# Sparse and cross attention: the low parts of the keys in both halves of the rows

## The chip, the cores and the metric

The kernel runs on one core of one Trainium2 chip. The metric is the device time of one execution in microseconds (us), the median of the runs shown; lower is better. Five engines work side by side, each on its own instruction queue: TensorE (PE; its weight loads are listed apart as PEld), VectorE (DVE), ScalarE (ACT), GpSimd (POOL) and SyncE (SP), which here only issues DMAs.

## The reference, cut to what matters

Two transformer blocks run one after the other on 256 tokens of width 1024, all in float32. The first block has a pooling mixer, a block attention and a gated MLP. The second has two layers, each with a mixer, a cross attention to 256 memory rows, an output projection with layer norm, and a mixture of 16 experts (MoE). The mixer of layer 0 is a sparse attention (NSA: 12 query heads of width 64, 4 key heads, a compressed, a selected and a window branch, mixed by gates); that of layer 1 is a latent attention (MLA). What this change is about is the scores:

- NSA, for each of 12 heads: the query times the keys of the selected and of the window branch, `s = (q · k) * 0.125`, causal, softmax, times the values, times the gate of the branch.
- Cross attention, in each layer, 4 heads of width 64: `s = (xq · mem_k) * 0.125`, softmax over the 256 memory rows, times `mem_v`.

## The kernel before, in words

**Split products.** TensorE takes a float32 product in two ways here: as float32 in several passes, or as fp32r in one pass with fewer bits. To keep the accuracy at one pass, an operand is split into a high part (its fp32r rounding) and a low part (what is left): `put_split` makes the high part with a copy (`copy`, on ACT or DVE, whichever the planner finds sooner) and the low part with a subtraction (`tt`, on DVE or POOL). A projection adds three products, high by high, high by low and low by high (`mm3`).

**Scores of heads of width 64.** A head has 64 rows, and the array has 128. `nsa_queries` (line 1480) and `cross` (line 1312) therefore put the high part of the query into one half of the rows and its low part into the other half, in one tile `qs`. `nsa` (line 1429) and `cross_keys` (line 1301) put the high part of the keys into both halves of `kh`. One matmul over 128 rows then gives high by high and low by high at once. A second matmul, over the 64 rows that hold the high query, multiplies it with the low part of the keys, `kl`, which lies in that half alone:

```python
nc.tensor.matmul(sv, q[:, i % 3, kv % 2, ts_], kh[:, kv, :, :nk], start=True, stop=False)
nc.tensor.matmul(sv, q[r, i % 3, kv % 2, ts_], kl[r, kv // 2, :, :nk], start=False, stop=False)
```

In `nsa_pair` (line 1500) a score group is these two and two bf16 matmuls that add the causal mask; a group covers 128 queries (`qt` is 0 or 1) and, for both branches at once, 2x128 or 2x256 keys. There are 12 heads and two groups each: 24 groups. In `cross`, `pair(j)` makes two groups, and each holds two heads: 128 rows, 64 rows, 128 rows, 64 rows, with 256 keys each. There are two pairs in each of two layers: 8 groups.

**Behind a score** stands `attend` (line 901): a maximum on DVE, small DVE operations, two exponentials on ACT, a reciprocal, two scalings (ACT, DVE or POOL), transposes on PE, a copy, and then the products with the values.

**The order of the work** is made by a planner in the kernel itself (class `Plan`): all operations are recorded in program order with an estimate of their time (`cost`), and `order` puts them on the engines one after the other, taking at each step the operation that can start first, with a preference for those that are due early (`rank`). `group()` keeps the matmuls of a group together. `filler(later)` makes what is recorded in it due later, so that it fills holes: in `nsa` that is, among others, the values, `cross_keys(0)`, the compressed branch and the second half of the queries; in `mla` `cross_keys(1)` and two thirds of the queries. `turn` books 0.19 us on PE where a matmul has at most 64 rows and the one in front of it has more, or the other way round, and 0.095 us for such a change in the columns. Where the planner sees a hole of over 0.6 us on PE, it puts matmuls on a dummy tile (`busy`, line 972 in the profile) into it, so that the engine stays busy. A tile's place in the arena (208 units of 256 columns) is given when its first operation is ordered; a DMA of MoE weights (512 KB, 4 units) is ordered when there is room for it.

Of the kernel before, what the change touches and what calls it, by code (L numbers as in the profile page):

```python
# [11 lines left out]
F32 = mybir.dt.float32  # L12
F32R = mybir.dt.float32r
# [3 lines left out]
OP = mybir.AluOpType  # L17
AX = mybir.AxisListType

S = 256  # L20
# [627 lines left out]
class K:  # L648
# [652 lines left out]
    def cross_keys(self, l):  # L1301

        mk = self.mem[l][0]
        kh, kl = self.mid([2, 2, S], F32R), self.mid([2, S], F32R)
        for j in range(2):
            r, o = self.halves(j), self.halves(1 - j)
            self.copy(kh[r, j], mk[r])
            self.tt(kl[r], mk[r], kh[r, j].bitcast(F32), OP.subtract)
            self.copy(kh[o, j], mk[r])
        return kh, kl  # L1310

    def cross(self, l, xq, keys, mixT):

        nc = self.nc
        mv, (kh, kl) = self.mem[l][1], keys
        qs = self.mid([2, 2, S], F32R)
        for j in range(2):
            r, o = self.halves(j), self.halves(1 - j)
            self.copy(qs[r, j], xq[r])
            self.tt(qs[o, j], xq[r], qs[r, j].bitcast(F32), OP.subtract)  # L1320

        def pair(j):
            r = self.halves(j)

            def score(qt):
                sv, ts_ = self.ps().rearrange("p (i k) -> p i k", i=2), slice(qt * 128, qt * 128 + 128)
                with nc.group():
                    for s in range(2):
                        nc.tensor.matmul(sv[:, s], qs[:, j, s, ts_], kh[:, j, s], start=True, stop=False)
                        nc.tensor.matmul(sv[:, s], qs[r, j, s, ts_], kl[r, s], start=False, stop=True)  # L1330
                return sv
            pt = self.attend(score, (256, 256), 0.125)
            o = self.ps()
            with nc.group():
                for kt in range(2):
                    for s in range(2):
                        h = 2 * j + s
                        nc.tensor.matmul(o[64 * s:64 * s + 64, :S], mv[:, kt, h * 64:h * 64 + 64], pt[:, s, 2 * kt:2 * kt + 2],
                                         start=(kt == 0), stop=(kt == 1))
            self.put_split(o[:, :S], mixT[0][:, 6 + j], mixT[1][:, 6 + j])  # L1340
        for j in range(2):
            pair(j)
# [86 lines left out]
    def nsa(self, x):  # L1429

        nc, A, h = self.nc, self.A, self.h
        W = A["nsa_w_in"]


        kh, kl = self.big([4, 2, S], F32R), self.mid([2, 2, S], F32R)
        kf = [self.mid([2, S]) for _ in range(2)]
        for br, c0 in ((0, 768 + 512), (1, 768 + 1024)):
            self.feat(W, c0, 256, h, lambda j, p: self.rope(p, kf[j][:, br], self.Cn, self.Sn, S))
        for j in range(2):
            for s in range(2):  # L1440
                r, o = self.halves(s), self.halves(1 - s)
                self.copy(kh[r, 2 * j + s], kf[j][r])
                self.tt(kl[r, j], kf[j][r], kh[r, 2 * j + s].bitcast(F32), OP.subtract)
                self.copy(kh[o, 2 * j + s], kf[j][r])
        q = [self.nsa_queries(0, W, h)]

        wg = self.load(W[:, 2304:2340].rearrange("(k p) f -> p k f", p=128), [8, 36])
        wv = self.split(wg, [8, 36])
        p = self.ps()
        for kk in range(2):  # L1450
            with nc.group():
                for k in range(4 * kk, 4 * kk + 4):
                    self.mm3(p[:36, :S], (wv[0][:, k], wv[1][:, k]), (h[0][:, k], h[1][:, k]), k == 0, k == 7)
        gT, gates = self.sml(), self.stay([128, 2, 12, 3], "gates")
        nc.scalar.activation(gT[:36], p[:36, :S], AF.Sigmoid)
        p = self.ps()
        with nc.group():
            for t in range(2):
                nc.tensor.transpose(p[:, t * 36:(t + 1) * 36], gT[:36, t * 128:(t + 1) * 128], self.ident[:36, :36])
        self.copy(gates, p[:, :72].rearrange("p (t h b) -> p t h b", t=2, h=12))  # L1460
        vs, xq = self.mid([2, 2, 256]), self.mid([2, S])
        with nc.filler(self.LATE):
            for br, c0 in ((0, 768 + 768), (1, 768 + 1280)):
                self.tok256(W, c0, h, lambda t, p: self.copy(vs[:, br, t], p))
            keys = self.cross_keys(0)
            kcz, vb = self.compressed(W, h)
            q.append(self.nsa_queries(1, W, h))
            self.feat(W, 2340, 256, h, lambda j, p: self.copy(xq[:, j], p), heads=True)
        mixT = self.hilo()
        for c in range(2):  # L1470
            PcT = self.sml()
            self.compressed_probs(c, q[c][0], kcz, gates, PcT)
            for j in range(3 * c, 3 * c + 3):
                self.nsa_pair(j, c, q[c][1], kh, kl, gates, PcT, vb, vs, mixT)
        self.cross(0, xq, keys, mixT)
        return self.out_ln(0, mixT)
# [23 lines left out]
    def nsa_pair(self, j, c, q, kh, kl, gates, PcT, vb, vs, mixT):  # L1500
        nc = self.nc
        PTs, heads = [], []
        for s in range(2):
            hd = 2 * j + s
            i = hd - 6 * c
            kv = hd // 3
            heads.append((i, kv))
            r = self.halves(kv % 2)

            def score(qt):  # L1510
                nk = 128 * (qt + 1)
                sv = self.ps().rearrange("p (i k) -> p i k", i=2)[:, :, :nk]
                with nc.group():
                    ts_ = slice(qt * 128, qt * 128 + 128)
                    nc.tensor.matmul(sv, q[:, i % 3, kv % 2, ts_], kh[:, kv, :, :nk], start=True, stop=False)
                    nc.tensor.matmul(sv, q[r, i % 3, kv % 2, ts_], kl[r, kv // 2, :, :nk], start=False, stop=False)
                    for b in range(2):
                        nc.tensor.matmul(sv[:, b, nk - 128:], self.identb, self.causalb, start=False, stop=(b == 1))
                return sv
            PTs.append(self.attend(score, (128, 256), 0.125, coef=lambda qt: gates[:, qt, hd, 1:3]))  # L1520
        o = self.ps()
        with nc.group():
            for s, (i, kv) in enumerate(heads):
                nc.tensor.matmul(o[64 * s:64 * s + 64, :S], vb[:96, c, i], PcT[:96], start=True, stop=False)
            for b in range(2):
                self.pv_causal(o, [vs[:, b, :, kv * 64:kv * 64 + 64] for _, kv in heads], [PTs[s][:, b] for s in range(2)],
                               start=False, stop=(b == 1))
        self.put_split(o[:, :S], mixT[0][:, j], mixT[1][:, j])
# [489 lines left out]
```

## Time and profile before

| | |
|---|---|
| Median of 3 runs | 1085.08 us (1084.48 to 1088.63) |
| The profiled execution | 1079.5 us, of which 1077.8 us are the span from the first to the last instruction |
| Mean granted TensorE clock | 0.993 |
| Busy share of the span | PE 97%, PEld 65%, DVE 54%, ACT 38%, POOL 6% |
| HBM read | 290.60 MB, 271 GB/s over the span |

The shares are means over stages with different limits: block 1 and its MLP last to about 320 us, NSA with cross attention and output to about 505 us, the first MoE to about 740 us, MLA with cross attention and output to about 840 us, the second MoE to the end. Matmuls are pipelined and their ends are modelled, so that a busy PE isn't one at its peak: what a matmul holds the engine for is read from one start to the next. Nearly every instruction is issued in one helper and has its line, L639; groups are told apart by tiles and shapes.

### The profile page before, as it was taken

The page shows a single profiled execution, that of the slowest core. Times are in us where ns is not written, and L with a number is a line of the kernel's source. Part 1 is how long each engine was busy: PE and PEld are TensorE (multiplying, and loading weights), DVE is VectorE, ACT ScalarE, POOL GpSimd, SP SyncE. Part 2 cuts the span into 40 slices and gives each one's busy share as a digit, 9 for nine tenths or more (in the row PEclk, how much of TensorE's full clock was granted, in tenths as well). Part 3 has the DMA queues.
Part 4 walks back from the last instruction along what each step waited for, and adds up shares of the span by engine and source line. Part 5 has one row for each costly group of instructions (what it writes and reads, how often), then busy time and mean ns, then how long its engine had stood idle before and what let it go on. Part 6 is the DMA issues. An engine that isn't in the chain of part 4 may idle for free. (4 is left out here: it accounts for less than half of the span.)

```text
span 1077.8 us, 16501 instructions
## 1 busy us (share of the span) xinstructions
PE 1047.4 (97%) x6169; PEld 696.5 (65%) x6169; DVE 580.1 (54%) x1514; ACT 412.0 (38%) x957; POOL 64.2 (6%) x68
## 2 busy tenths in 40 slices
PE   9999999999999999999999999999999999999995
PEld 5987999999988887777333443436877434443431
DVE  7699997867765899885221111107995412110103
ACT  4484673534344566574211111215763312111211
POOL 0231100000010000200000000002200100000000
PEclk9999999999999999899999999999999999999998
DMA  9995235464676441287999999999677799999994
GB/s 309 362 330 199 95 117 178 146 223 164 243 235 199 172 157 60 70 292 262 333 387 374 368 387 367 365 350 378 226 258 272 245 385 371 363 387 379 355 356 149
DMA packets 172356, 292.83 MB, mean 272 GB/s; under 512 B 9251, under 2 KB 59340, under 8 KB 172268
## 3 DMA queue, kind: packets, MB, share of 16 engines
q1 hardware_dynamic: 172268, 291.69, 77.1%
q8 instruction: 51, 0.84, 0.3%
q14 instruction: 37, 0.30, 0.1%
HBM read 290.60 MB, written 1.06 MB: 271 GB/s over the span
## 5 line engine op out<-in xcount | busy, mean ns | idle before, releaser
L639 PE MATMUL ps<-span,span 128*128 128x256 f32 (+6 forms) x5432 | 948.7, 397 | 6.2 <-DVE span L639 3.0
L639 PEld LDWEIGHTS ps<-span,span 128*128 128x128 f32 (+2 forms) x5432 | 624.0, 173 | 305.2 <-issue 238.0
L639 DVE TENSOR_TENSOR span<-span,span 128x512 fp32r<-128x512 f32 (+6 forms) x415 | 244.9, 631 | 20.4 <-ACT span L639 18.4
L639 ACT CAST span<-span 128x512 fp32r<-128x512 f32 (+5 forms) x320 | 166.0, 574 | 23.6 <-DVE span L639 11.1
L639 DVE TENSOR_TENSOR span<-ps,span 128x512 fp32r<-128x512 f32 (+3 forms) x104 | 56.6, 550 | 176.4 <-ACT span L639 110.1
L639 DVE SCALAR_TENSOR_TENSOR span<-span,tiny,ps 128x512 f32<-128x512 f32 x16 | 12.0, 747 | 192.8 <-PE ps L639 192.8
L639 POOL TENSOR_TENSOR span<-span,span 128x512 fp32r<-128x512 f32 (+4 forms) x37 | 49.5, 1351 | 968.5 <-ACT span L639 592.0
L639 ACT COPY span<-ps 128x512 f32<-128x512 f32 (+3 forms) x109 | 53.1, 495 | 134.1 <-PE ps L639 119.5
L639 ACT CAST span<-ps 128x512 fp32r<-128x512 f32 (+1 forms) x67 | 34.2, 513 | 164.3 <-PE ps L639 150.1
L639 PE MATMUL ps<-cst,span 128*128 128x128 f32 (+1 forms) x363 | 59.5, 283 | 10.9 <-DVE span L639 8.8
L639 ACT ACTIVATE span<-ps 128x512 f32<-128x512 f32 (+3 forms) x33 | 18.5, 561 | 113.3 <-PE ps L639 113.0
L639 PEld LDWEIGHTS ps<-cst,span 128*128 128x128 f32 (+1 forms) x363 | 40.0, 141 | 30.5 <-DVE span L639 16.9
L639 ACT ACTIVATE span<-span 128x256 f32<-128x256 f32 (+4 forms) x36 | 16.1, 451 | 98.7 <-DVE span L639 94.9
L639 ACT ACTIVATE span<-ps,tiny 128x256 f32<-128x256 f32 (+3 forms) x94 | 42.9, 467 | 21.5 <-DVE tiny L639 17.0
L639 ACT ACTIVATE span<-ps,vecs 128x256 f32<-128x256 f32 (+2 forms) x62 | 29.4, 511 | 53.8 <-PE ps L639 53.5
L639 ACT ACTIVATE span<-span,tiny 128x256 f32<-128x256 f32 (+3 forms) x59 | 30.2, 531 | 20.4 <-DVE tiny L639 20.2
L639 DVE TENSOR_REDUCE tiny<-ps 64x1 f32<-64x2 f32 (+3 forms) x78 | 30.3, 393 | 12.2 <-PE ps L639 10.4
L972 PE MATMUL ps<-busy 128*128 128x512 bf16 x122 | 30.7, 404 | 1.4 <-POOL busy L968 1.4
L639 DVE TENSOR_SCALAR span<-ps,vecs 128x256 f32<-128x256 f32 (+2 forms) x25 | 13.1, 526 | 32.8 <-ACT span L639 32.6
L639 DVE CAST span<-span 128x512 fp32r<-128x512 f32 (+7 forms) x79 | 29.4, 381 | 2.1 <-DMA span<-in_w_in_dram 1.0
L639 PE MATMUL ps<-span,cst 8*128 8x512 f32 (+1 forms) x48 | 25.5, 625 | 0.0
L639 DVE SCALAR_TENSOR_TENSOR span<-span,vecs,span 128x255 f32<-128x255 f32 (+2 forms) x52 | 24.4, 481 | 0.7
(106 smaller groups left out, 368.5 us busy)
## 6 DMA issues: line engine op xcount, KB each, us to landing
span<-in_moe_w_gate_dram SPq DMA_DIRECT2D x128, 512.0 KB, 6.5
span<-in_moe_w_up_dram SPq DMA_DIRECT2D x128, 512.0 KB, 7.7
span<-in_moe_w_down_dram SPq DMA_DIRECT2D x128, 512.0 KB, 6.8
span<-in_w_up_dram SPq DMA_DIRECT2D x22, 1024.0 KB, 5.2
span<-in_w_out_dram SPq DMA_DIRECT2D x12, 1024.0 KB, 10.5
span<-in_w_down_dram SPq DMA_DIRECT2D x11, 1024.0 KB, 5.1
span<-in_w_in_dram SPq DMA_DIRECT2D x7, 1024.0 KB, 9.6
span<-in_nsa_w_in_dram SPq DMA_DIRECT2D x7, 1024.0 KB, 8.3
```

What stands on the lines that cost most here:

```text
L639: getattr(eng, op)(*[real(x) for x in a], **{n: real(x) for n, x in k.items()})
L972: return lambda: nc.nc.tensor.matmul(nc.banks[bank], busy[:, :128], busy, start=True, stop=True)
```

## The change

The low part of the keys is put into both halves of the rows, and the second matmul of a score goes over all 128 rows. It then adds the high and the low part of the query, each times the low part of the keys. For this `kl` in `nsa` becomes two tiles of [2, 2, 256] (one for each pair of key heads) in place of one, and in `cross_keys` it becomes [2, 2, 256] in place of [2, 256]. A copy to the other half comes after each subtraction: four in `nsa`, two in each call of `cross_keys`. The number of matmuls, their columns and their order within a group stay as they were.

```diff
@@ cross_keys
-        kh, kl = self.mid([2, 2, S], F32R), self.mid([2, S], F32R)
+        kh, kl = self.mid([2, 2, S], F32R), self.mid([2, 2, S], F32R)
         for j in range(2):
             r, o = self.halves(j), self.halves(1 - j)
             self.copy(kh[r, j], mk[r])
-            self.tt(kl[r], mk[r], kh[r, j].bitcast(F32), OP.subtract)
+            self.tt(kl[r, j], mk[r], kh[r, j].bitcast(F32), OP.subtract)
             self.copy(kh[o, j], mk[r])
+            self.copy(kl[o, j], kl[r, j].bitcast(F32))
         return kh, kl
@@ cross
-            r = self.halves(j)
-
...
-                        nc.tensor.matmul(sv[:, s], qs[r, j, s, ts_], kl[r, s], start=False, stop=True)
+                        nc.tensor.matmul(sv[:, s], qs[:, j, s, ts_], kl[:, j, s], start=False, stop=True)
@@ nsa
-        kh, kl = self.big([4, 2, S], F32R), self.mid([2, 2, S], F32R)
+        kh, kl = self.big([4, 2, S], F32R), [self.mid([2, 2, S], F32R) for _ in range(2)]
...
                 self.copy(kh[r, 2 * j + s], kf[j][r])
-                self.tt(kl[r, j], kf[j][r], kh[r, 2 * j + s].bitcast(F32), OP.subtract)
+                self.tt(kl[j][r, s], kf[j][r], kh[r, 2 * j + s].bitcast(F32), OP.subtract)
                 self.copy(kh[o, 2 * j + s], kf[j][r])
+                self.copy(kl[j][o, s], kl[j][r, s].bitcast(F32))
@@ nsa_pair
-            r = self.halves(kv % 2)
...
-                    nc.tensor.matmul(sv, q[r, i % 3, kv % 2, ts_], kl[r, kv // 2, :, :nk], start=False, stop=False)
+                    nc.tensor.matmul(sv, q[:, i % 3, kv % 2, ts_], kl[kv // 2][:, kv % 2, :, :nk], start=False, stop=False)
```

## Rows read from the trace of the kernel before

**Rows 1.** The page: busy time of each engine; the chain that ended last.
```profile
PE 1047.4 (97%) x6169; PEld 696.5 (65%) x6169; DVE 580.1 (54%) x1514; ACT 412.0 (38%) x957; POOL 64.2 (6%) x68
...
issue 9%; PE 4%; DMA 1%; POOLq 0%; DVE 0%; DVEq 0%
```

**Rows 2.** Busy time by stretch: stretch, length, each engine, clock, DMA share, GB/s.
```profile
60.00:100.00 40.00, 40.00 (x238) 31.84 (x237) 39.88 (x108) 24.80 (x59) 10.79 (x13) 1.00 0.83 274
...
390.00:420.00 30.00, 29.35 (x257) 24.47 (x256) 26.55 (x106) 17.19 (x54) 1.45 (x1) 1.00 0.18 61
...
450.00:480.00 30.00, 29.73 (x204) 20.98 (x205) 26.80 (x88) 22.82 (x79) 4.51 (x4) 1.00 0.76 264
...
760.00:832.00 72.00, 71.01 (x465) 58.26 (x464) 57.38 (x155) 40.90 (x120) 6.69 (x5) 1.00 0.72 252
```

**Rows 3.** Timeline of PE, NSA: start, length, instruction, first shape, count.
```profile
400.08 3.11 PE L639 MATMUL ps<-span,span 128*128 128x256 f32 x24
403.03 0.27 PE L639 MATMUL ps<-cst,span 128*128 128x128 f32 x1
...
416.00 0.90 PE L639 MATMUL ps<-span,span 128*128 128x512 f32 x2
416.84 0.29 PE L639 MATMUL ps<-bfs 128*128 128x128 bf16 x2
416.93 0.68 PE L639 MATMUL ps<-span,span 128*128 128x256 f32 x2
417.54 0.28 PE L639 MATMUL ps<-bfs 128*128 128x128 bf16 x2
...
477.29 11.05 PE L639 MATMUL ps<-span,span 128*128 128x512 f32 x50
488.18 1.03 PE L639 MATMUL ps<-cst,span 128*128 128x128 f32 x8
```

**Rows 4.** PE's 64-row matmuls by shape: two of 300 to 520, one of 720 to 860.
```profile
L639 PE MATMUL ps<-span,span 64*128 64x256 f32 x20 | 8.0, 400 | 0.0
...
L639 PE MATMUL ps<-span,span 64*128 64x512 f32 x12 | 6.2, 520 | 0.0
...
L639 PE MATMUL ps<-span,span 64*128 64x256 f32 x8 | 3.0, 380 | 0.0
```

**Rows 5.** Timeline of PE: two score groups of the first cross attention.
```profile
466.66 2.55 PE L639 MATMUL ps<-span,span 128*128 128x256 f32 x8
469.14 1.09 PE L639 MATMUL ps<-cst,span 128*128 128x128 f32 x8
```

**Rows 6.** Timeline of PE, NSA: where PE stood or was kept busy.
```profile
365.72 2.55 PE L972 MATMUL ps<-busy 128*128 128x512 bf16 x11
369.23 0.69 PE L639 MATMUL ps<-span,span 128*128 128x256 f32 x2 [0.96 <-DVE span L639]
...
389.20 0.41 PE L639 MATMUL ps<-cst,span 128*128 128x128 f32 x2 [1.40 <-DVE span L639]
...
441.20 0.77 PE L639 MATMUL ps<-cst,span 128*128 128x128 f32 x2 [1.03 <-ACT span L639]
```

**Rows 7.** 361 to 366: its busy time by engine, and its 64-row copies.
```profile
361.00:366.00 5.00, 5.00 (x43) 4.84 (x42) 4.83 (x11) 4.52 (x9) 0.00 (x0) 1.00 0.00 1
...
L639 ACT CAST span<-span 64x512 fp32r<-64x512 f32 x6 | 3.7, 619 | 0.4 <-DVE span L639 0.3
...
L639 DVE CAST span<-span 64x512 fp32r<-64x512 f32 x2 | 0.8, 422 | 0.0
```

**Rows 8.** Busy time by stretch, where the clock fell.
```profile
440.00:445.00 5.00, 3.97 (x15) 2.31 (x13) 3.52 (x19) 2.54 (x7) 0.36 (x1) 0.56 0.00 0
445.00:450.00 5.00, 5.00 (x31) 4.40 (x30) 3.41 (x16) 2.85 (x14) 0.00 (x0) 0.76 0.00 0
```

**Rows 9.** Busy time by stretch: before the first MoE, and in it.
```profile
505.00:510.00 5.00, 4.99 (x36) 3.49 (x35) 4.66 (x16) 2.41 (x5) 0.00 (x0) 1.00 0.05 8
520.00:720.00 200.00, 198.17 (x922) 78.62 (x920) 28.94 (x56) 31.71 (x57) 2.49 (x2) 1.00 1.02 371
```

## The prediction

> **What bounds the kernel now.** I read the page first: PE is busy 97% of the span, no other engine over 54%, and the chain that ended last is PE, "issue" and a little DMA [rows 1]. So an amount of PE time taken out can count, if PE is what the stage waits for. That is read stage by stage, from the busy times by stretch [rows 2]. In NSA, 390 to 420 us and 450 to 480, PE is busy 29.35 and 29.73 of 30 us, but DVE stands close behind it, at 26.55 and 26.80, while ACT has 17.19 and 22.82. From 760 to 832, which holds the second cross attention, PE has 71.01 of 72, DVE 57.38, ACT 40.90. Both stages are PE's by a short head in NSA and a long one in MLA. Since a busy PE may be one that waits inside a modelled matmul, I then read the timeline of PE from start to start.
>
> There the reader is to see a gap in rate. In a projection, 24 matmuls of 256 columns over 128 rows go by from 400.08 to 403.03, 0.123 us each, and 50, mostly of 512 columns, from 477.29 to 488.18, 0.218 us each [rows 3]. A score pair of the same columns, 128 rows and then 64 rows, takes 416.84 − 416.00 = 0.84 us for two of 512 columns and 417.54 − 416.93 = 0.61 us for two of 256 [rows 3]. In cross attention, where the two kinds alternate, 8 matmuls of 256 columns take 469.14 − 466.66 = 2.48 us, 0.310 each [rows 5]. Nothing is waited for in these groups, as no idle time is listed. What the slow ones have in common is a change between 128 and 64 rows: it costs 0.84 − 2 x 0.218 = 0.404 us for two changes, 0.61 − 2 x 0.123 = 0.364 for two, and 0.310 − 0.123 = 0.187 for one.
>
> **The change, part by part.** *The changes of rows go.* Of the 20 matmuls of 64 rows and 256 columns in the NSA stage 12 are NSA's short groups and 8 cross attention's; the 12 of 512 columns are NSA's long groups; 8 more stand in the second cross attention [rows 4]. So: 12 x 0.404 = 4.8 us, 12 x 0.364 = 4.4, 16 x 2 x 0.187 = 6.0, which halves into 3.0 for each layer. PE is relieved of 4.8 + 4.4 + 3.0 = 12.2 us in the NSA stage and of 3.0 in MLA, 15.2 together. The matmuls themselves cost the same: their columns and their number stay, and the 128-row ones of the projections are the price that I have put in.
>
> Here a rule speaks against the change. What the rows show is that a pair of 128 and 64 rows holds PE longer than two of 128 rows, and not shorter, in all three kinds of group [rows 3, 5]. The Trainium skill, "TensorEngine Tiling (Array Packing)", When to Use Tiling, advises tiles of 64 rows for contractions of up to 64, for up to twice the speed; by it, giving the low products all 128 rows is a step back. The same page, Key Properties, says that a change of the tiling mode drains the array, and with that the 0.187 us agree. By the first rule the low products would lose up to half of their streaming time, an estimate of 12 x 0.109 + 28 x 0.062 = 3.0 us; by the second the sum stays as above.
>
> *How much of the 12.2 us NSA keeps.* Its lower end is nothing: DVE could be what the stage then waits for. Its upper end is 12.2. What DVE allows, if no operation leaves it, is its idle time: 3.45 + 3.20 us in the two stretches of 30 [rows 2] and 1.48 + 1.59 between 440 and 450 [rows 8], 9.7 in all of the 70 us. DVE can run full: 39.88 of 40 us from 60 to 100 [rows 2]. And part of its work, copies and scalings, can go to ACT, which has 7 to 13 idle us in each stretch of 30. The holes of PE that are there already won't shrink, as they end on DVE and ACT: 2.55 of dummy matmuls and 0.96, then 1.40, then 1.03 [rows 6]. I take 8.1, two thirds, which is nearest to what DVE's own idle time allows, less some for the chains in which maximum, exponential and scaling follow each other.
>
> *The four copies in NSA.* One takes 0.62 us on ACT or 0.42 on DVE [rows 7]. They fall where the keys are split, 361 to 366, and there DVE is busy 4.83 of 5 us and ACT 4.52 [rows 7]. Two engines that share them need about 4 / (1/0.42 + 1/0.62) = 1.0 us. Behind them on both queues wait the ropes and splits of the first queries, and for those PE waits: the dummy matmuls and the hole before 369.23 [rows 6]. So they cost 1.0, at the most 4 x 0.62 = 2.5, and 0 if the planner slips them behind the queries; the first score needs them only at 369.
>
> *The two copies of each `cross_keys`* are due late and have ACT's idle time for cover, at worst 4 x 0.62 = 2.5 us for both layers if ACT were full. I take 0.
>
> *The room.* Four more units stand taken through NSA and two more from each `cross_keys` on, of 208. What waits for room are the loads of the MoE weights, 4 units each. One load fewer in advance is 0.5 MB at 371 GB/s, 1.4 us [rows 9]. Between 505 and 510 the DMA share is 0.05 [rows 9]: the loads stand complete before the MoE starts, and NSA's keys are free by then. So 0, at worst twice 1.4. No DMA is added or moved, on SP's queue or POOL's.
>
> *MLA.* PE relieved of 3.0 us; DVE has 14.6 idle us of 72 there. I take 2.5, between 0 and 3.0.
>
> **The sum.** −8.1 + 1.0 − 2.5 = −9.6 us. Against the profiled execution, 1079.5, that is 1069.9. The median of the runs shown lies 5.6 above that execution, and so I put the median after at 1085.08 − 9.6 = 1075.5.
>
> **The rivals.**
>
> *A. DVE and the chains take over (0.17).* PE then waits where it worked. For it: DVE is at 88% in NSA, and every hole there ends on DVE or ACT [rows 6]. Against it: ACT's idle time and DVE's 39.88 of 40 elsewhere. NSA would keep perhaps 2 of its 12.2, less 1.0 for the copies: with MLA's 2.5 some −3.5, 1081.6.
>
> *B. The MoE takes it back (0.06).* Its weights come at 371 GB/s with a DMA share of 1.02 [rows 9]; an earlier start helps only if the loads start earlier too. Against it: they were complete at 505 with time to spare. MoE would return all of NSA's 7.1, leaving 2.5: 1082.6.
>
> *C. The clock falls more often (0.10), the case on the slower side.* After PE stood 1.03 us before 441.20 [rows 6], with thin work around it, the granted clock was 0.56 and then 0.76 of full for 5 us each, the lower level of 1.2 GHz for part of the time [rows 8]: 5 x 0.44 + 5 x 0.24 = 3.4 us, with the hole 4.4. A PE that is done sooner while DVE is not has more such holes, and they lie where the late fillers are used up, 440 to 470. With four more of them than before: 4 x 4.4 − 9.6 = +8.0, 1093.1. Up to two they leave it level, from four on it is slower by over 0.5%. For it: the clock did fall there once. Against it: the planner fills the holes that it foresees, and full matmuls in place of drained ones keep PE denser. The Trainium skill, "TensorE: Matmul & The Clock Gate", Part 1, has it that the lower rate is the default and that steady work releases the higher one; the trace agrees, with these two stretches.
>
> *D. The change doesn't remove the slow steps (0.03).* If a second matmul on the same bank with the same weights were slow for another reason, 128 rows would not help; and if 64 rows had been the cheaper form, they would cost up to half of the low products' streaming, 12 x 0.218 / 2 + 28 x 0.123 / 2 = 3.0 us, more. Against it: the projections add to one bank, too, at 0.123 [rows 3]. Then the copies count and up to 3.0: +1.0 to +4.0, 1086.1 to 1089.1. (That is the time that the skill's page on array packing would give.)
>
> **How the numbers follow.** The forecast has 0.64 and reaches from all that the rows allow, −15.2 + 0 (1069.9), to a gain of 5.4 (1079.7). A new order is also planned from the first changed operation on, and that moves holes like those of [rows 6] by some us either way, so the low end goes to 1067. At the top A, B and the cheap end of D lie within, up to 1086.1, and I stop at 1087; C and the rest of D above it and a little below 1067 are left out. About 0.5%, 5.4 us, is what a measurement of this kernel can tell from no change. Faster by more is the forecast, 0.64; within it are A, B and D, 0.26; slower is C, 0.10.
>
> **What would show it.** In the profile after, no matmul of 64 rows is left from 300 to 520 and from 720 to 860; a score pair in NSA takes about 0.44 and 0.25 us from start to start, and the 8 of cross attention about 1.0. The first score comes about 1 us later than 369.23, the first MoE's stretch starts some 7 us earlier, the second's some 10. It is wrong in size if PE's idle time and dummy matmuls between 360 and 500 grow by more than about 5 us, and wrong in sign if the clock falls in several stretches there.

## The result, and the profile after

The changed kernel takes 1073.86 us, the median of 4 runs (1070.42 to 1075.42). The kernel before, run beside it, takes 1084.78 (4 runs, 1083.28 to 1088.63). The ratio is 0.9889, with a 95% interval of 0.9866 to 0.9912: 1.1% faster. The forecast was 1075.5, in a range of 1067 to 1087. The profiled execution takes 1070.42, with a span of 1068.7, which is 9.1 less than the profiled one before.

The page's busy times, which answer to [rows 1]:

```profile
PE 1034.6 (97%) x6168; PEld 691.8 (65%) x6175; DVE 580.8 (54%) x1526; ACT 413.9 (39%) x954; POOL 61.2 (6%) x67
```

PE's time fell by 12.8 us, that of DVE and ACT together rose by 2.6, and no share has moved by more than a point. Twelve DVE instructions more, three ACT ones fewer and one POOL one fewer: eight copies, and four operations that the planner gave to DVE.

No matmul of 64 rows is left in the NSA stage or in MLA's ([rows 4] before). The timeline of PE in NSA, which answers to [rows 3]; start, length, first shape and count:

```profile
410.60 0.48 PE L639 MATMUL ps<-span,span 128*128 128x256 f32 x2
410.92 0.28 PE L639 MATMUL ps<-bfs 128*128 128x128 bf16 x2
411.01 0.71 PE L639 MATMUL ps<-span,span 128*128 128x512 f32 x2
411.57 0.28 PE L639 MATMUL ps<-bfs 128*128 128x128 bf16 x2
```

From start to start a short pair takes 0.32 us where it took 0.61, a long one 0.56 where it took 0.84. That is less of a gain than forecast (0.25 and 0.44 were expected). Read one by one, the second matmul of a pair, which has its own kind in front of it and a mask behind, now holds the engine for 0.122 or 0.238 us, about the rate of a projection. The first one still takes 0.202 or 0.318: it stands behind a mask or a transpose, which are no fp32r matmuls, and some 0.09 us at that seam are left. In cross attention a matmul inside a run of score groups takes 0.117 to 0.121 us, as forecast.

Where PE stood, in the same stage ([rows 6] before):

```profile
366.15 2.55 PE L972 MATMUL ps<-busy 128*128 128x512 bf16 x10
369.66 0.50 PE L639 MATMUL ps<-span,span 128*128 128x256 f32 x2 [0.96 <-DVE span L639]
389.80 0.50 PE L639 MATMUL ps<-cst,span 128*128 128x128 f32 x2 [1.78 <-DVE span L639]
...
440.49 0.79 PE L639 MATMUL ps<-cst,span 128*128 128x128 f32 x5 [0.31 <-DVE span L639]
441.63 0.51 PE L639 MATMUL ps<-span,span 128*128 128x256 f32 x2 [0.35 <-ACT span L639]
...
444.26 0.43 PE L639 MATMUL ps<-cst,span 128*128 128x128 f32 x2 [0.87 <-DVE span L639]
...
451.59 0.81 PE L972 MATMUL ps<-busy 128*128 128x512 bf16 x2
```

The first score comes at 369.66, 0.43 us later than before (0.7 counted from the first rope), with the four copies in front of it. The holes are a little longer and there are more of them around 440. Yet the clock did not fall there. The same stretches as [rows 8], and one in the MoE where it fell instead (columns as in [rows 2]):

```profile
440.00:445.00 5.00, 3.47 (x19) 2.09 (x19) 4.81 (x22) 3.52 (x17) 0.00 (x0) 1.00 0.01 2
445.00:450.00 5.00, 5.00 (x47) 4.13 (x48) 5.00 (x26) 3.76 (x17) 0.00 (x0) 1.00 0.09 23
...
660.00:665.00 5.00, 5.00 (x20) 1.56 (x18) 0.15 (x1) 0.59 (x1) 0.00 (x0) 0.70 1.05 385
```

**The time by stage.** I cut every run at events that it has: the first shuffle of a rope, the first routing matmul on `selb`, the first mask of MLA, the routing matmul of layer 1. The NSA stage runs from the first to the second, the first MoE to the third, MLA to the fourth. Of the kernel before:

```profile
355.80:506.20 150.40, 145.63 (x1046) 118.73 (x1046) 125.95 (x415) 90.55 (x259) 9.59 (x13) 0.98 0.47 165
506.20:766.50 260.30, 254.35 (x1270) 115.64 (x1269) 70.69 (x163) 64.82 (x136) 13.33 (x10) 1.00 1.01 362
766.50:837.30 70.80, 70.34 (x455) 56.20 (x453) 56.00 (x163) 39.96 (x113) 2.54 (x2) 1.00 0.64 223
```

and of the changed one:

```profile
355.60:496.70 141.10, 134.59 (x1049) 115.50 (x1052) 125.54 (x427) 88.45 (x252) 8.96 (x13) 1.00 0.56 197
496.70:760.30 263.60, 257.00 (x1274) 116.66 (x1275) 71.37 (x163) 65.07 (x138) 13.28 (x10) 0.99 0.99 355
760.30:828.30 68.00, 67.49 (x454) 55.16 (x453) 55.46 (x163) 40.01 (x113) 2.54 (x2) 1.00 0.68 240
```

NSA is 9.3 us shorter, the first MoE 3.3 longer, MLA 2.8 shorter; ahead of NSA 0.2 and behind MLA 0.1 us went. That is the 9.1 of the span. So the first MoE starts 9.5 us earlier, where some 7 were expected, and the second 9.0, where some 10 were. PE's idle time in the NSA stage, its length less the busy time, grew from 4.8 to 6.5 us.

Two things are open from here. One is how much of the 9.3 is PE's relieved time and how much the clock: in [rows 8] the clock took 3.4 us, and after it takes none. The other is luck: a changed kernel gets a wholly new plan, and another order of the same work might be worth as much.

### The profile page after: what moved, and what is told of

It reads as the page before. It is cut to its first block, busy times and chain, and to the rows that moved or that the text cites. A ratio compares the mean times of both kernels' runs of the same rounds, so it can differ in the third digit from the quotient of the medians.

```text
span 1068.7 us, 16521 instructions
## 1 busy us (share of the span) xinstructions
PE 1034.6 (97%) x6168; PEld 691.8 (65%) x6175; DVE 580.8 (54%) x1526; ACT 413.9 (39%) x954; POOL 61.2 (6%) x67
## 5 line engine op out<-in xcount | busy, mean ns | idle before, releaser
L639 PE MATMUL ps<-span,span 128*128 128x256 f32 (+5 forms) x5432 | 937.5, 397 | 7.3 <-ACT span L639 3.8
L639 DVE TENSOR_TENSOR span<-span,span 128x512 fp32r<-128x512 f32 (+7 forms) x418 | 248.2, 633 | 18.5 <-ACT span L639 15.1
L639 ACT CAST span<-span 128x512 fp32r<-128x512 f32 (+4 forms) x317 | 166.3, 574 | 35.4 <-PE ps L639 12.7
L639 POOL TENSOR_TENSOR span<-span,span 128x512 fp32r<-128x512 f32 (+3 forms) x34 | 45.1, 1340 | 894.4 <-ACT span L639 329.1
L639 PE MATMUL ps<-cst,span 128*128 128x128 f32 (+2 forms) x363 | 58.8, 281 | 11.4 <-DVE span L639 10.2
L639 PEld LDWEIGHTS ps<-cst,span 128*128 128x128 f32 (+2 forms) x363 | 40.3, 140 | 30.2 <-DVE span L639 16.6
L639 DVE CAST span<-span 128x512 fp32r<-128x512 f32 (+6 forms) x90 | 34.0, 384 | 2.6 <-DMA span<-in_w_in_dram 1.9
```

The lines of the kernel that those rows point to most:

```text
L639: getattr(eng, op)(*[real(x) for x in a], **{n: real(x) for n, x in k.items()})
```

## The experiments

Twelve kernels ran, each beside the kernel before on the same chip. The table has all of them. "Clock loss" is the sum over stretches of 5 us of 5 x (1 − granted clock) in the NSA stage of the profiled execution: the most that the lower level can have cost there. The last two columns take in the whole program and every execution of which the span and the mean granted clock are known (89 of the kernel before, 4 to 12 of each other): "whole loss" is the mean of span x (1 − clock), again the most that the clock can have cost. Among the 89, 1 us more of it goes with 0.87 us more of time. Times in us.

| kernel | ratio to before (95%) | NSA stage | clock loss in it | less the loss | MLA stage | whole loss | mean span less it |
|---|---|---|---|---|---|---|---|
| before | 1 | 150.4 | 3.4 | 147.0 | 70.8 | 14.0 | 1069.0 |
| n1_before_hop | 1.0027 (1.0008 to 1.0047) | 149.0 | 3.5 | 145.5 | 71.4 | 11.1 | 1075.3 |
| n2_before_near | 1.0018 (0.9988 to 1.0048) | 154.9 | 8.5 | 146.4 | 73.6 | 15.6 | 1070.1 |
| changed | 0.9889 (0.9866 to 0.9912) | 141.1 | 0 | 141.1 | 68.0 | 9.6 | 1062.1 |
| n3_after_hop | 0.9929 (0.9904 to 0.9953) | 142.5 | 0 | 142.5 | 68.0 | 9.7 | 1065.6 |
| n4_after_near | 0.9953 (0.9937 to 0.9970) | 143.9 | 1.7 | 142.2 | 68.9 | 11.5 | 1066.2 |
| e1_nsa_only | 0.9984 (0.9965 to 1.0004) | 146.6 | 0 | 146.6 | 71.7 | 9.9 | 1071.1 |
| e2_cross_only | 0.9949 (0.9930 to 0.9968) | 145.2 | 3.4 | 141.8 | 69.5 | 14.6 | 1062.1 |
| e3_copies_only | 1.0087 (1.0060 to 1.0114) | 156.6 | 12.0 | 144.6 | 70.8 | 21.6 | 1069.1 |
| e7_copies_other_order | 1.0054 (1.0031 to 1.0078) | 156.4 | 12.0 | 144.4 | 72.2 | 22.1 | 1067.9 |
| e8_twice_the_changes | 1.0137 (1.0107 to 1.0167) | 167.8 | 17.1 | 150.7 | 72.4 | 26.0 | 1073.6 |
| e5_low_side_by_side | 1.0002 (0.9986 to 1.0017) | 149.4 | 3.5 | 145.9 | 69.6 | 13.2 | 1069.1 |
| e4_blind_plan | 1.0006 (0.9984 to 1.0028) | 150.4 | 5.1 | 145.3 | 70.9 | 14.0 | 1068.6 |
| e6_less_weights | 0.9850 (0.9810 to 0.9890) | 141.2 | 1.5 | 139.7 | 67.9 | 9.6 | 1056.7 |

### What an order alone is worth: n1 to n4

The same work in other orders, got by moving one constant of the planner a little, in the kernel before and in the changed one:

```diff
-    HOP = 0.2
+    HOP = 0.205
```
```diff
-    NEAR = 0.08
+    NEAR = 0.085
```

n1_before_hop:

> The kernel before with one constant of the planner moved by a fortieth (HOP 0.205 for 0.2): the same work in another order. It measures what an order alone is worth: within 3 us of before, ratio 0.997 to 1.003, if order is noise beside the row changes; a move of 8 us or more would make luck of the order a rival for the whole gain.

n2_before_near:

> The kernel before with another constant of the planner moved (NEAR 0.085 for 0.08): again another order of the same work; within 3 us of before, ratio 0.997 to 1.003, by the theory of the row changes.

n3_after_hop:

> The changed kernel with HOP 0.205 for 0.2. Row changes: the gain stays, ratio to before 0.986 to 0.992. Luck of the order: it comes back towards before, 0.995 or more.

n4_after_near:

> The changed kernel with NEAR 0.085 for 0.08. Row changes: the gain stays, ratio to before 0.986 to 0.992. Luck of the order: 0.995 or more.

The orders of the kernel before lie within 0.3% of each other. Of the changed kernel's, one kept 0.7% of the 1.1% and one 0.47%; the second is just over the line that I had drawn for luck, and neither is as fast as the change itself or lies in the 0.986 to 0.992 that was expected. So an order is worth up to 0.6% here, and the change got a good one. Over three orders each, the mean is (1 + 1.0027 + 1.0018) / 3 = 1.0015 before and (0.9889 + 0.9929 + 0.9953) / 3 = 0.9924 after: 0.9% faster. All three changed ones beat all three of before, and by stage the sets don't overlap: NSA 141.1 to 143.9 against 149.0 to 154.9, MLA 68.0 to 68.9 against 70.8 to 73.6. About half of what differs within a set lies elsewhere: the stretch ahead of the first rope, which the change doesn't touch, ends at 355.6 in the changed kernel, at 359.3 in n3 and at 360.4 in n4.

The orders are of two kinds. In n1, n3, n4, e3 and e7 the first score of NSA comes 30 to 32 us after the first rope, in all others 13 to 15. The gain is there in both: less the clock loss, the NSA stage takes 147.0 and 146.4 before and 141.1 changed with early scores, and 145.5 before (n1) and 142.5 and 142.2 changed with late ones.

The whole program answers the question of the clock. Over the three orders each, the mean loss is (14.0 + 11.1 + 15.6) / 3 = 13.6 us before and (9.6 + 9.7 + 11.5) / 3 = 10.3 after, and the span less it is 1071.5 before and 1064.6 after. So up to 3.3 us of some 10 are the clock's, and 6.9 are not.

### One part alone: e1, e2

e1_nsa_only is the changed kernel with `cross_keys` and `cross` as before:

```diff
-        kh, kl = self.mid([2, 2, S], F32R), self.mid([2, 2, S], F32R)
+        kh, kl = self.mid([2, 2, S], F32R), self.mid([2, S], F32R)
...
-                        nc.tensor.matmul(sv[:, s], qs[:, j, s, ts_], kl[:, j, s], start=False, stop=True)
+                        nc.tensor.matmul(sv[:, s], qs[r, j, s, ts_], kl[r, s], start=False, stop=True)
```

> NSA's low products over 128 rows, cross attention as before. If the gain is the row changes taken off PE, this keeps NSA's part of it: 9.2 of the 15.2 us, of which some two thirds count, less 1.0 for the copies: 4 to 8 us faster than before, ratio 0.993 to 0.996, and the cross groups still take 2.5 us for 8 matmuls. If the gain were luck of a new order, the time could lie anywhere between before and after or outside, with no tie to the 9.2.

e2_cross_only is the kernel before with those lines as changed:

```diff
-                        nc.tensor.matmul(sv[:, s], qs[r, j, s, ts_], kl[r, s], start=False, stop=True)
+                        nc.tensor.matmul(sv[:, s], qs[:, j, s, ts_], kl[:, j, s], start=False, stop=True)
```

> Cross attention's low products over 128 rows, NSA as before. Row changes: 3.0 us off PE in each layer, so 3 to 6 us faster than before, ratio 0.9945 to 0.997; the MLA stage loses about 2.8 as in the full change. Luck of order: no tie to 6.0, and MLA's stage need not get shorter.

Cross attention alone came as expected in the total, 0.5%. Its MLA stage is 69.5, only 1.3 us shorter where some 2.8 were expected; of the rest a fall of the clock at 830 to 840 (0.78 and 0.88) can explain 1.7. NSA alone fell short: 0.16%, an interval that holds 1, where 0.4 to 0.7% were expected. The score groups are as short in it as in the changed kernel, so PE was relieved, and the stage did not keep it. Its NSA stage is 3.8 us shorter, which is just the clock loss of before; less that, nothing is left (146.6 against 147.0), and MLA is as before at 71.7. The two don't add up by stage: without the clock, cross attention's share took 5.2 us off the NSA stage, where it frees 3.0 of PE, and NSA's took 0.4, where it frees some 7. One order of each is too little to split the stage between them, given the spread of n1 to n4. The whole program is as lopsided: less the loss, e1 is 2.1 us longer than the kernel before and e2 6.9 us shorter. How much of the gain is NSA's stays open. The sum of both ratios' gains, 0.67%, is a bit under the 0.9% of the mean of orders.

### The copies alone: e3, e7

The changed kernel with all copies and tiles, but the second matmuls over 64 rows as before:

```diff
-                        nc.tensor.matmul(sv[:, s], qs[:, j, s, ts_], kl[:, j, s], start=False, stop=True)
+                        nc.tensor.matmul(sv[:, s], qs[r, j, s, ts_], kl[r, j, s], start=False, stop=True)
...
-                    nc.tensor.matmul(sv, q[:, i % 3, kv % 2, ts_], kl[kv // 2][:, kv % 2, :, :nk], start=False, stop=False)
+                    nc.tensor.matmul(sv, q[r, i % 3, kv % 2, ts_], kl[kv // 2][r, kv % 2, :, :nk], start=False, stop=False)
```

> The low parts stand in both halves (all eight copies and the tiles are kept), but the second matmuls go over 64 rows as before. Row changes: nothing is gained and the copies cost about 1.0 us, at the most 2.5 in NSA: ratio 1.000 to 1.003. If the gain came from the other order that the copies bring, it would stay: 0.99.

It came out 0.9% slower, far over the price of the copies, and neither theory had that. The windows say where. Busy time by stretch of e3 (clock third from the end):

```profile
440.00:445.00 5.00, 5.00 (x22) 2.94 (x22) 4.91 (x30) 2.91 (x13) 1.09 (x3) 0.59 0.00 0
445.00:450.00 5.00, 5.00 (x21) 3.23 (x20) 4.09 (x17) 2.67 (x11) 0.00 (x0) 0.50 0.01 2
450.00:455.00 5.00, 5.00 (x18) 2.80 (x16) 4.25 (x20) 3.41 (x15) 0.00 (x0) 0.50 0.00 2
455.00:460.00 5.00, 5.00 (x35) 3.51 (x35) 2.21 (x9) 1.84 (x8) 0.00 (x0) 0.70 0.86 290
475.00:480.00 5.00, 5.00 (x14) 3.61 (x14) 3.92 (x15) 3.56 (x14) 1.43 (x1) 0.50 1.05 388
480.00:485.00 5.00, 5.00 (x29) 3.94 (x28) 1.34 (x5) 2.30 (x5) 0.00 (x0) 0.81 0.75 261
```

PE is listed as busy in all of them, without a hole, and the clock is at the lower level for much of 20 us and again later. Its timeline there is score group upon score group:

```profile
445.00 1.07 PE L639 MATMUL ps<-span,span 128*128 128x256 f32 x2
446.00 0.39 PE L639 MATMUL ps<-bfs 128*128 128x128 bf16 x2
446.16 1.07 PE L639 MATMUL ps<-span,span 128*128 128x256 f32 x2
447.16 0.39 PE L639 MATMUL ps<-bfs 128*128 128x128 bf16 x2
447.35 1.06 PE L639 MATMUL ps<-cst,span 128*128 128x128 f32 x4
448.06 1.50 PE L639 MATMUL ps<-span,span 128*128 128x512 f32 x2
449.49 0.40 PE L639 MATMUL ps<-bfs 128*128 128x128 bf16 x2
```

A pair of 256 columns takes 1.00 us here, from 446.16 to 447.16, where it took 0.61 at the full clock. To part the copies from the clock, e7 is e3 with `NEAR` at 0.085:

> The copies alone again (low products over 64 rows), with NEAR 0.085 for 0.08, so in another order. The first one was 9 us slower than before with 12 us of lower clock in the NSA stage. If the copies themselves cost some 1 us and the rest was the clock, the NSA stage less its clock loss is again 144 to 148 us long, whatever the clock does, and the total moves with the clock loss. If the copies cost 9 us, the stage is over 150 also without the clock loss.

The total is 0.5% slower. The clock fell at the same places, 12.0 us, so this was a weak test of what the clock does; but less the clock the stage is 144.4 us, not over 150. The copies don't cost 9 us. Less the loss, both stages are even shorter than the kernel before's 147.0, and little apart from the 145.5 of n1, which has late scores as they do, and no copies. In the whole program less its loss e3 and e7 lie at 1069.1 and 1067.9 and the kernel before at 1069.0. So the copies cost about nothing, give or take some 1 us (an order moves more than that, and the loss is the most that the clock can have cost), and the slowdown goes with the clock. Why these two lost more clock than n1, with as many changes of rows, no run shows.

### Twice the changes of rows: e8

The kernel before, with the low product of an NSA group cut into its two branches, and a mask behind each:

```diff
-                    nc.tensor.matmul(sv, q[r, i % 3, kv % 2, ts_], kl[r, kv // 2, :, :nk], start=False, stop=False)
                     for b in range(2):
+                        nc.tensor.matmul(sv[:, b], q[r, i % 3, kv % 2, ts_], kl[r, kv // 2, b, :nk], start=False, stop=False)
                         nc.tensor.matmul(sv[:, b, nk - 128:], self.identb, self.causalb, start=False, stop=(b == 1))
```

> The kernel before, with each NSA score group's 64-row matmul cut into its two branches and a mask behind each: the same columns, four changes of rows in a group in place of two, 24 x 0.39 = 9.3 us more on PE. If changes of rows cost PE time and a part of it counts, as in the forecast, the NSA stage less its clock loss grows by 3 to 8 us. If drained matmuls also let the clock fall, its clock loss grows over the 3.4 us of before. If neither, the stage stays at about 147 us and the loss at 3.4.

Both parts of the expectation came: 1.4% slower, the stage 17.4 us longer than the kernel before's; 3.7 of that stand without the clock, and the clock loss went from 3.4 to 17.1. The whole program says the same over all executions: 12.0 us more of loss, and 4.6 us more without it. Three stretches of it and the whole stage:

```profile
410.00:425.00 15.00, 14.82 (x72) 9.69 (x70) 10.69 (x48) 8.01 (x27) 0.00 (x0) 0.66 0.13 36
445.00:465.00 20.00, 19.99 (x86) 13.22 (x85) 15.02 (x69) 11.73 (x47) 1.57 (x5) 0.57 0.11 36
485.00:495.00 10.00, 10.00 (x37) 6.79 (x37) 5.62 (x18) 5.27 (x19) 2.62 (x2) 0.66 0.99 353
355.40:523.20 167.80, 164.50 (x1068) 131.04 (x1070) 131.80 (x428) 88.27 (x250) 5.84 (x9) 0.90 0.43 147
```

PE is busy 14.82 of 15, 19.99 of 20 and 10 of 10 us while the clock is down. More changes of rows, more clock lost, with hardly any idle time listed to account for it. (The cut also adds a weight load and a matmul to each group; the columns are the same.)

### The change of rows or the narrow matmul: e5

The kernel before, with the two narrow matmuls of a cross group side by side:

```diff
-                    for s in range(2):
-                        nc.tensor.matmul(sv[:, s], qs[:, j, s, ts_], kh[:, j, s], start=True, stop=False)
-                        nc.tensor.matmul(sv[:, s], qs[r, j, s, ts_], kl[r, s], start=False, stop=True)
+                    nc.tensor.matmul(sv[:, 0], qs[:, j, 0, ts_], kh[:, j, 0], start=True, stop=False)
+                    nc.tensor.matmul(sv[:, 0], qs[r, j, 0, ts_], kl[r, 0], start=False, stop=True)
+                    nc.tensor.matmul(sv[:, 1], qs[r, j, 1, ts_], kl[r, 1], start=True, stop=False)
+                    nc.tensor.matmul(sv[:, 1], qs[:, j, 1, ts_], kh[:, j, 1], start=False, stop=True)
```

> The kernel before, with the four matmuls of a cross group in the order 128, 64, 64, 128 rows: as many narrow matmuls as before, but two changes of rows in place of four. If the change of rows is what costs, a group takes some 0.86 us in place of 1.24, 8 groups 3.0 us less, and the kernel is 1.5 to 3 us faster, ratio 0.997 to 0.9985. If the narrow matmul itself is slow, the group stays at 1.24 us and the ratio at 1.

One group of MLA's cross attention and the start of the next, matmul by matmul:

```profile
805.06 0.28 PE L639 MATMUL ps<-span,span 128*128 128x256 f32 x1
805.26 0.38 PE L639 MATMUL ps<-span,span 64*128 64x256 f32 x1
805.49 0.28 PE L639 MATMUL ps<-span,span 64*128 64x256 f32 x1
805.70 0.38 PE L639 MATMUL ps<-span,span 128*128 128x256 f32 x1
805.92 0.28 PE L639 MATMUL ps<-span,span 128*128 128x256 f32 x1
```

To the nanosecond the starts are 805.057, 805.265, 805.488, 805.695 and 805.919. The group takes 0.862 us from start to start, the 0.86 expected: the change of rows is what costs, 0.185 us each ((0.862 − 4 x 0.123) / 2). Each of the four matmuls stands beside one change. The one just before a change holds PE for 0.208 us at 128 rows and 0.207 at 64, the one just after a change for 0.224 at 128 and 0.223 at 64, where 0.12 is the rate without changes. So a change costs the matmul on either side of it some 0.09 to 0.10 us, and 64 rows are here no slower and no faster than 128. In the kernel before each matmul of a run of groups had a change on both sides, and took 0.310. The time as a whole didn't move, 1.0002. MLA's stage is 1.2 us shorter than before's, NSA's 1.0, and the rest of the new order gave it back: the first MoE is 5.3 us longer.

### A plan that doesn't know: e4

The changed kernel; for the second matmuls the planner is told 64 rows and books the changes that are gone (`low` isn't passed to the chip):

```diff
-        return a[1].shape[0] <= 64, a[0].shape[0] <= 64
+        return k.get("low", False) or a[1].shape[0] <= 64, a[0].shape[0] <= 64
```

> The changed kernel, but the planner books the second matmuls as if they still had 64 rows, 0.38 us and more a group that PE no longer spends. If PE's saved time counts by itself, the engines run ahead of the plan and most of the gain stays: ratio to before 0.989 to 0.993. If the gain needs an order that is planned for it, PE waits at the places that the plan has set for other engines: 0.995 or more, with more idle time of PE in NSA.

The second branch: 1.0006, nothing is left of the gain. PE's waits in the NSA stage of e4, by what ended them (total, times, longest):

```profile
PE ps L639 <- DVE span L639: 5.5, 10, 1.1
PE ps L639 <- ACT span L639: 1.8, 5, 0.6
PE ps L639 <- DVE tiny L639: 1.1, 2, 0.9
PE ps L639 <- DVE kcz L639: 0.5, 1, 0.5
```

and in that of the changed kernel:

```profile
PE ps L639 <- DVE span L639: 4.9, 8, 1.8
PE ps L639 <- DVE selb L639: 0.9, 1, 0.9
PE ps L639 <- ACT span L639: 0.4, 1, 0.4
```

8.9 us of waits against 6.2, and the clock fell where PE stood (5.1 us). In the whole program 6.5 us are lost to the changed kernel also without the clock. So here the matmuls that got shorter behind the planner's back left PE waiting. This is one order; how far another blind one would lie from it wasn't tried, but its distance to the changed kernel, 1.2%, is nearly twice that of n4, 0.64%.

### The pace of the first MoE: e6

The changed kernel; in the last pair of experts of the first MoE both use the weights of the first of the two, which leaves 6.3 MB of loads out and changes what these experts compute:

```diff
-                    ws_ = [self.chunk(A[w_][l, 2 * pr + e], 128 * k, 256, 0, 512) for e in range(2)]
+                    ws_ = [self.chunk(A[w_][l, 2 * pr + e], 128 * k, 256, 0, 512) for e in range(1 if (l, pr) == (0, 7) else 2)] * 2
```

> The changed kernel; in the last pair of experts of the first MoE both experts use the weights of one, so 6.3 MB of loads are left out and all matmuls stay. If the first MoE goes at the pace of its loads, 6.3 MB at 371 GB/s are up to 17 us, cut off where PE takes over: 4 us or more faster than the changed kernel. If PE sets the pace, it stays within 1.5 us of it.

The ratio to before is 0.9850 where the changed kernel has 0.9889, some 4 us less. The stage from the first routing to MLA's first mask:

```profile
498.90:756.70 257.80, 253.96 (x1270) 115.86 (x1269) 70.77 (x163) 64.32 (x136) 13.00 (x10) 1.00 0.95 341
```

257.8 us against 263.6, of which 1.7 are the clock's fall at 655 to 665 that this run doesn't have. The intervals of the two ratios overlap; the stage is the better witness, as it takes 260.3 to 265.6 us in all the other kernels. So some 4 us hang on the loads, of the 17 that 6.3 MB take: loads and PE are close there, and the loads come last by a little.

## Why the prediction was right, point by point

**The total** was right, 9.6 us forecast against 10.9 in the median, and 9.1 between the profiled executions. Over three orders it is 0.9%, some 10 us. The cause is the one named, the changes of rows on PE: e8 doubles them in NSA and the kernel gets slower, e5 halves them in cross attention and the groups get shorter by what was worked out (though the kernel as a whole does not), and the copies without the wider matmuls bring nothing. That the size fits so well is in part luck. The NSA stage kept less of PE's time than forecast, and the clock, which the sum did not have, made up for it.

**MLA** was forecast at −2.5 and came at −2.8. The mean of its three orders is 68.3 after and 71.9 before, −3.6, of which one clock fall in n2 is about 1.

**NSA** was forecast at −8.1 + 1.0 = −7.1 and came at −9.3, by terms that were mis-sized both ways:

- *The relieved time* was 12 x 0.404 + 12 x 0.364 for the score groups of NSA. It measured 0.84 − 0.56 = 0.28 and 0.61 − 0.32 = 0.29, 6.8 us in place of 9.2. The step that failed is the base: I took the rate inside a projection for both matmuls of a pair, but the first has another kind of matmul in front of it and keeps some 0.09 us of that seam. In cross attention, where a group stands behind a group, the base held: 0.185 us a change in e5, against 0.187.
- *What is kept of it.* Less the clock, the mean of the three orders went from (147.0 + 145.5 + 146.4) / 3 = 146.3 to (141.1 + 142.5 + 142.2) / 3 = 141.9. That is 4.4 net of the copies, not 7.1. PE's idle time grew, and 4.9 of the 6.2 us of its listed waits end on DVE, which points to rival A, in part. Of 6.8 + 3.0 us of PE that came off, less than half was kept.
- *The clock* had no term in the sum, and rival C had it with the wrong sign. It gave 3.4 us in this pair, and in the mean of three orders (3.4 + 3.5 + 8.5) / 3 = 5.1 before against (0 + 0 + 1.7) / 3 = 0.6 after. Rival C expected more falls, from more holes. There are more holes after, and fewer falls. These are single executions; by all of them the clock is worth up to 3.3 us in the whole program.

**The copies** were put at 1.0 us, between 0 and 2.5. The first score is 0.43 us later, and less the clock e3 and e7 are 0.1 us longer and 1.1 shorter than the kernel before. That fits a cost between 0 and 1, and another order moves more.

**The room** was put at 0, and the loads were complete again when the first MoE started at 496.7: the DMA share is 0.14 from 500 to 505 in the changed kernel. **The first MoE** is 3.3 us longer, which the sum didn't have. Of this 1.7 are a clock fall at 655 to 665. For the rest: before's 260.3 is the shortest of all runs with the full loads (261.6 to 265.6 in the others), and e6 shows that its loads come last by a little. The mean of three orders is 263.9 after and 261.8 before, 2.1 longer, of which 1.7 go with falls of the clock there. So rival B, with 7.1 us given back, didn't happen, though its mechanism, a MoE that goes at the pace of its loads, is there in e6.

**Rival D** fell with the timeline: the slow steps are gone but for the seam. Nor were 64 rows the cheaper form: in e5 a matmul of 64 rows holds PE as long as one of 128 in the same place.

## What to carry to other kernels

Look at matmuls from start to start, not at their durations: a short matmul between others with another number of rows held the engine for 0.31 us where its like took 0.12, and a copy that cost next to nothing bought it back. Where a planner or a hand-made order rules, tell it about the new cost: the one plan that didn't know of the relief lost all of it (e4). And before a gain of 1% is believed, run the same work in two or three other orders, and take the clock of every execution into account: here one order was worth half of the gain and the clock up to a third.

## What the runs showed of the hardware that I had not expected

- The granted clock falls without any idle time listed on PE. In e3 it is at 0.50 from 445 to 455 with PE busy 5.00 of 5 us, in score groups that change between 128 and 64 rows; in e8, with twice the changes, 17.1 us of the NSA stage are lost, nearly all of it that way. In the changed kernel, with no changes of rows, PE stood for 1.5 us of 440 to 445 and the clock stayed at 1.00. Over all kernels the loss in the NSA stage is 3.4 to 17.1 us in the eight whose NSA scores change rows, and 0, 0, 0, 1.5, 1.7 and 5.1 in the six whose don't. So the falls tend to go with the changes of rows, and the two sets overlap: e4, with none, lost 5.1 where PE stood. By what the chip goes, no run shows. The clock also fell in the MoE with PE busy (0.70 at 660 to 665), and at another place in other runs.
- A change between 128 and 64 rows costs the matmul on either side of it: with 256 columns 0.208 us in front of a change and 0.224 behind one (e5), 0.310 between two (before) and 0.12 with none.
- An fp32r matmul behind a bf16 mask or a float32 transpose takes some 0.09 us more than behind its like (0.202 against 0.122 in the changed kernel).
